# Residual quarters given back to the residual three slabs, one slab and two jobs earlier, and the last transposes one step later, in a two-layer decoder in fp32

## The chip, the core and the metric

The kernel runs on one core of a Trainium2 chip. TensorE (PE) multiplies and transposes, VectorE (DVE) and ScalarE (ACT) do the element-wise work, GpSimd (POOL) does a little of it and issues some DMAs, and SyncE (SP) issues nearly all the others. The metric is the device time of one execution, in microseconds; the profile gives the span of the recorded instructions, which is a little shorter.

## What is computed

A causal decoder trunk of two layers over 256 tokens of width 2048, all in fp32. The part that the change touches is the squared-ReLU feed-forward block at the end of each layer:

```python
def squared_relu_mlp(h, w1, w2):
    z = jax.nn.relu(h @ w1)
    return (z * z) @ w2

for i in range(DEPTH):                       # DEPTH = 2
    ...
    x = x + jnp.concatenate([token_out, mem_out], axis=-1) @ w_out[i]
    x = x + squared_relu_mlp(rms_norm(x, ffn_norm[i]), w_ff1[i], w_ff2[i])
```

`w_ff1` is 2048 x 8192 and `w_ff2` 8192 x 2048. Layer 0 mixes tokens by pooling, layer 1 by differential attention; both have a memory cross-attention.

## The kernel before

**Weights.** All large weights stand in DRAM as one array `in_w` of 725 rows of 128 x 1024, in the order in which they are used. `Feed.load` (L126) brings them in: one DMA of SP per row (L147), into a "raw" row (plain blocks, four buffers) or a "slab" row. To keep fp32 accuracy, a row is split in two: ACT casts it to fp32r (`hi`, L178), DVE subtracts that from the row (`lo`, L181), both into a ring of six half-row slots (`hi_ring`, `lo_ring`; two more slots, `slot`, in the feed-forward block). PE then makes three products of high and low parts. `_prepare` (L185) runs three preparations ahead of the matmuls, and `load` three rows ahead of that.

**Slabs.** Most of `w_ff2` (both halves A and B of its columns) is multiplied by a scheme of seven products in place of eight for a block of 2 x 2. A slab is two rows, a and b, and four jobs, j = 0 to 3 (`slab_jobs`, L1003; matmuls L1031 to L1033 into seven PSUM banks `p`). Row a needs more than a load: when it has landed, POOL issues a DMA (L149) that adds the second half of row b onto it. ACT's cast of the row comes behind that, then DVE subtracts (L209) and, for row b, adds (L212).

**Borrowed buffers.** Slab rows rotate over three buffers (tag `rows`) and over those in `feed.more`: in the feed-forward block that is the four quarters a to d of the residual (tags `resida` to `residd`), which is copied to DRAM (`kept`, L853) for that time. `load` counts rows and takes the buffer by the count modulo 3 + the number of borrowed ones. `reload` (L855) takes a quarter back and issues its DMA from `kept` (L860) on SP; like any load, that DMA first waits until the last row in this buffer has been read.

**Order of the block.** `ffn` (L835) runs up tiles (`h @ w1`, a bank `x_bank`, matmuls L940 and L942, emptied by ACT's copy at L954) with the slab jobs in between, in seven phases that alternate between the halves: the last but one, LAST-1, is half B, slabs 16 to 23, and LAST is half A, slabs 20 to 31. At the end of a phase `finish_banks` (L1047) combines the seven banks into four corners (`c_x`, `c_y` and `room`, or `c_a` and `c_b`). Corners of a phase that doesn't end its half are parked in DRAM (`part`); at LAST two DMAs (L1158) fetch them into two free places of the buffers `za` and `zb`, and DVE's L409 scales the new corners and adds the parked ones. Last, `turn(h)` transposes corners on PE (`ct`, L1100) and DVE adds them to the residual (L1103). Small pieces of such work are put off by `at(n, ...)` until n steps later; a step (`tick`) comes every four blocks.

**What sets the order.** The program is written as one sequence. The framework's scheduler sorts each engine's instructions, except those pinned to the order of the program, and each engine then runs its own queue in order: an instruction that waits holds up what stands behind it. SP's queue holds all loads, reloads, fetches and parks one behind the other.

**Places of the change.** In `go` (L1139) four of them are tied to a slab and a job: after job 3 of slab 22 of LAST-1, `feed.more` is cut to quarters c and d (L1150); after job 3 of slab 22 of LAST, a and b are reloaded (L1152); after job 3 of slab 28, borrowing ends and the parked corners are fetched (L1154); after job 1 of slab 31, c and d are reloaded (L1161). The fifth is in `finish_banks`: at LAST, `turn(h)` comes 7 + h steps later (L1117).

Of the kernel before, what the change touches and what calls it, by code (L numbers as in the profile page):

```python
# [293 lines left out]
NB = 24  # L294
# [3 lines left out]
LAST = len(PHASES) - 1  # L298
# [65 lines left out]
def program(ctx, tc, plan, dry, xT, memT, par, lam, cst, wst, yT):  # L364
# [18 lines left out]
    def at(d, fn, rank=0):  # L383
        pend.setdefault(now[0] + d, []).append((rank, fn))

    def tick():
        now[0] += 1
        for _, fn in sorted(pend.pop(now[0], []), key=lambda r: r[0]):
            fn()
# [9 lines left out]
    def bk(tag, name, shape=(P, 512)):  # L399
        return pp.tile(list(shape), F32, tag=tag, bufs=1, name=name)  # L400
# [3 lines left out]
    def mmt(name):  # L404
        turnm[0] += 1
        return bk(f"m{(turnm[0] - 1) % 3}", name)

    def stt(out, a, s, b, op0, op1, **kw):
        nc.vector.scalar_tensor_tensor(out=out, in0=a, scalar=s, in1=b, op0=op0, op1=op1, **kw)  # L409
# [425 lines left out]
    def ffn(l, xs, tag, done):  # L835
# [19 lines left out]
        def reload(tags):  # L855
            for i in tags:
                assert f"resid{i}" not in feed.lent.values()
                j = "abcd".index(i)
                resid.parts[j] = resid_part(i, f"resid{i}{l}")
                nc.sync.dma_start(resid.parts[j], kept[:, 4 * j : 4 * j + 4, :])  # L860
# [5 lines left out]
        def take():  # L866
            return spare.pop(0)
# [80 lines left out]
        def up_tile(j, ps):  # L948
            narrow(ps, "w_ff1", j, list(range(NK)), lambda k: xs[:, k, :])
            if j == 1:  # L950
                r2c.append(columns("x")[1])
                r2.append(rstd_from("x"))
                nc.scalar.activation(r2[0], r2[0], AF.Square)
            nc.scalar.copy(pairs[j // 2 % 3][:, 512 * (j % 2) : 512 * (j % 2) + 512], ps)  # L954
            if j % 2:
                convert(j // 2, (1, 1, 2, 2, 3, 4, 5, 6) if j == 63 else STEPS)
# [43 lines left out]
        def bank():  # L1000
            return pp.tile([P, 512], F32, tag="st", bufs=1, name="x_bank")
# [38 lines left out]
        def open_banks():  # L1040
            ms = [f"m{(turnm[0] + i) % 3}" for i in range(3)]
            for p, tag in enumerate((*ms, "n0", "n1", "o", "t")):
                banks.append(bk(tag, f"p{p}"))
# [3 lines left out]
        def finish_banks(p):  # L1047

            half, begin, end = PHASES[p]
            p1, p7, p6, p2, p3, p4, p5 = banks  # L1050
            banks.clear()
            if p == LAST:
                upp, low = (
                    tp.tile([P, 2, 512], F32, tag="rows", bufs=3, name=f"c_{x}") for x in "ab"
                )
                x0, x2 = upp[:, 0, :], upp[:, 1, :]
            else:
                low = room[:, 3072:4096].rearrange("p (a c) -> p a c", a=2)
                x0 = tp.tile([P, 512], F32, tag="acc2", bufs=1, name="c_x")
                x2 = tp.tile([P, 512], F32, tag="rowsq", bufs=1, name="c_y")  # L1060
            x3, x1 = low[:, 0, :], low[:, 1, :]
            corners = ((x0, x2), (x3, x1))
            add, sub = nc.vector.tensor_add, nc.vector.tensor_sub
            nc.scalar.copy(x0, p1)
            nc.scalar.copy(x1, p5)
            sub(x2, x0, p6)
            add(x3, x2, p7)
            add(x0, x0, p2)
            add(x2, x2, x1)
            add(x2, x2, p3)  # L1070
            add(x1, x1, x3)
            add(x3, x3, p4)
            whole = end == (32 if half == "A" else NB)
            sides = ((x0, 0), (x2, 1), (low, slice(2, 4)))
            old = part.pop(half, None) if p < LAST else None

            def scale():
                for side, t in ((x0, 0), (x2, 0), (low, 1)):
                    grown = nc.scalar.activation(
                        side, side, AF.Copy, scale=r2c[0][:, t : t + 1]  # L1080
                    )
                    if not dry:
                        tc.keep_in_program_order(grown)

            def gather():
                for side, c in sides:
                    nc.gpsimd.dma_start(side, old[:, c, :], accum_op=ALU.add)

            def park():
                for side, c in sides:  # L1090
                    nc.sync.dma_start(part[half][:, c, :], side)

            def turn(h):
                c = 2 * h + 8 * (half == "A")
                t4 = bk(("t", "o", "n0", "n1")[h] if half == "A" else "st", "ct", (P, 2, T))
                for e in range(2):
                    n = (2 * h + e) // 4
                    w = (2 * h + e) % 4 * P
                    for t in range(2):
                        nc.tensor.transpose(  # L1100
                            t4[:, e, t * P : t * P + P], corners[t][n][:, w : w + P], ident
                        )
                sums = nc.vector.tensor_add(resid[:, c : c + 2, :], resid[:, c : c + 2, :], t4)  # L1103
                if not dry:
                    tc.keep_in_program_order(sums)
                if half == "A":
                    done(c)
                    done(c + 1)

            if p == LAST:  # L1110
                for t, side in enumerate((upp, low)):
                    stt(
                        side, side, r2c[0][:, t : t + 1], fetched[t].bitcast(F32),
                        ALU.mult, ALU.add,
                    )
                for h in range(4):
                    at(7 + h, lambda h=h: turn(h))  # L1117
                return
            if old is not None:
                at(10, gather)  # L1120
            if not whole:
                part[half] = dp.tile([P, 4, 512], F32, tag=f"part{half}{begin}", name=f"part{l}{p}")
                at(6 if old is None else 17, park)
                if p == LAST - 2:
                    at(15, scale)
                return

            at(15, scale)
            turns.append(turn)
# [9 lines left out]
        def go(some):  # L1139
            for at_, what in some:  # L1140
                if what[0] == "s":
                    p, i, j = what[1:]
                    if not banks:
                        open_banks()
                    if (p, i) not in runs:
                        runs[p, i] = slab_jobs(p, i)
                    runs[p, i](j)
                    if at_ < first_down and at_ >= ups:
                        tick()
                    if (p, i, j) == (LAST - 1, NB - 2, 3):  # L1150
                        feed.more = feed.more[2:]
                    if (p, i, j) == (LAST, 22, 3):  # L1152
                        reload("ab")
                    if (p, i, j) == (LAST, 28, 3):  # L1154
                        feed.more = []
                        for t in range(2):
                            fetched.append(spots[take()])
                            nc.sync.dma_start(  # L1158
                                fetched[t].bitcast(F32), part["A"][:, 2 * t : 2 * t + 2, :]
                            )  # L1160
                    if (p, i, j) == (LAST, 31, 1):  # L1161
                        reload("cd")
                    continue
                if what[0] == "turn":
                    turns[0](what[1])
                    continue
                if what[0] == "end":
                    finish_banks(what[1])
                    ends[0] = True
                    continue  # L1170
                if at_ == len(items) - 3:
                    feed.extra = None
                ps = bank() if banks or ends[0] else mmt("ff")
                ends[0] = None
                if what[0] == "f":
                    up_tile(what[1], ps)
                else:
                    feed.rows_whole = False
                    down_tile(*what[1:], ps)

        first_down = items.index(("d", 3, 0))
        items = list(enumerate(items))
        go(items[:ups])

        def last():
            go(items[ups:])
            feed.rows_whole = False
# [469 lines left out]
    for c in range(3):  # L1657
# [5 lines left out]
        for i in range(2):  # L1663
            j = 2 * c + i
# [10 lines left out]
    for h in range(4):  # L1675
# [5 lines left out]
            lambda c, h=h: [mvs[:, b, c, h * P : h * P + P] for b in range(2)],  # L1681
# [110 lines left out]
```

## Time and profile before

| | |
|---|---|
| median of 3 runs | 2016.76 us (2016.6 to 2017.52) |
| the profiled execution | 2016.9 us |
| its span | 2014.8 us |
| mean granted clock of TensorE | 0.998 |
| bytes read from DRAM by the core | 430.85 MB |

The page of the profile lists each engine's busy time, then the span in slices, DMA queues, the chain of work that ended last, the costliest groups of instructions, and DMA issues with the median time to landing. In rows of instructions, the first two numbers are the start in the span and the length, in us; then follow the engine, the line, the operation, result<-source by the program's names without their numbers, and the shape; in square brackets stands the idle time of the engine just before it and what ended it. "SPq" and "POOLq" are the issues of DMAs by those engines. A group of waits reads "who waited <- for whom: total us, times, longest". A row of a stretch reads from:to and length, then busy time with the number of instructions of PE, PEld (loading of weights), DVE, ACT and POOL, then the granted clock, the share of DMA time and GB/s.

### The profile page before, as it was taken

The page shows a single profiled execution, that of the slowest core. Times are in us where ns is not written, and L with a number is a line of the kernel's source. Part 1 is how long each engine was busy: PE and PEld are TensorE (multiplying, and loading weights), DVE is VectorE, ACT ScalarE, POOL GpSimd, SP SyncE. Part 2 cuts the span into 40 slices and gives each one's busy share as a digit, 9 for nine tenths or more (in the row PEclk, how much of TensorE's full clock was granted, in tenths as well). Part 3 has the DMA queues.
Part 4 walks back from the last instruction along what each step waited for, and adds up shares of the span by engine and source line. Part 5 has one row for each costly group of instructions (what it writes and reads, how often), then busy time and mean ns, then how long its engine had stood idle before and what let it go on. Part 6 is the DMA issues. An engine that isn't in the chain of part 4 may idle for free.

```text
span 2014.8 us, 30574 instructions
## 1 busy us (share of the span) xinstructions
PE 2002.6 (99%) x10592; PEld 1708.5 (85%) x10592; DVE 1785.1 (89%) x2705; ACT 1374.1 (68%) x2213; POOL 172.2 (9%) x203
## 2 busy tenths in 40 slices
PE   9999999999999999999999999999999999999999
PEld 7888888888888888888888899888888888888787
DVE  8888779999999999999875798879999999999898
ACT  7765567676666677677665698556666666776664
POOL 0001300001011111000000000410001010011000
PEclk9999999999999999999999999999999999999999
DMA  8556768779788887766665645767778888788674
GB/s 310 183 193 213 246 206 239 233 234 265 231 252 247 238 254 233 232 195 196 222 194 190 193 142 176 241 224 231 242 226 259 239 222 269 230 258 239 197 240 149
DMA packets 139403, 452.39 MB, mean 225 GB/s; under 512 B 15792, under 2 KB 18864, under 8 KB 139248
## 3 DMA queue, kind: packets, MB, share of 16 engines
q1 hardware_dynamic: 119520, 412.68, 61.3%
q0 software_dynamic: 19584, 37.76, 11.3%
q8 instruction: 83, 1.36, 0.3%
q14 instruction: 72, 0.59, 0.1%
q10 hardware_dynamic: 144, 0.01, 0.0%
HBM read 430.85 MB, written 16.78 MB: 222 GB/s over the span
## 4 chain that ended last, share of the span: by engine, by line
PE 96%; DVE 1%; ACT 1%; DMA 1%; issue 0%; SPq 0%; ACTq 0%; DVEq 0%; POOLq 0%
PE x_bank L940 23%; PE x_bank L942 11%; PE p L1031 9%; PE p L1032 9%; PE p L1033 9%; PE wo L519 6%; PE wo L521 3%; PE q L550 3%; PE k L550 3%; PE v L550 3%; PE ff L940 3%; PE u L519 2%; PE mk L550 2%; PE mv L550 2%; PE ff L942 1%; PE u L521 1%
## 5 line engine op out<-in xcount | busy, mean ns | idle before, releaser
L181 DVE TENSOR_TENSOR lo_ring<-raw,hi_ring 128x512 fp32r<-128x512 f32 (+1 forms) x675 | 565.2, 853 | 100.0 <-ACT hi_ring L178 93.0
L178 ACT CAST hi_ring<-raw 128x512 fp32r<-128x512 f32 (+1 forms) x675 | 493.1, 745 | 228.9 <-PE wo L519 62.0
L181 DVE TENSOR_TENSOR lo_ring<-slab,hi_ring 128x1024 fp32r<-128x1024 f32 (+1 forms) x332 | 343.0, 1045 | 35.9 <-ACT hi_ring L178 32.3
L178 ACT CAST hi_ring<-slab 128x1024 fp32r<-128x1024 f32 (+1 forms) x332 | 301.0, 907 | 68.5 <-DVE slab L212 37.0
L149 POOL DMA_DIRECT2D slab<-in_w x112 | 96.9, 865 | 1631.3 <-PE o_t L1649 344.5
L940 PE MATMUL x_bank<-fx,hi_ring 128*128 128x512 f32 x720 | 227.1, 396 | 0.0
L178 ACT CAST slot<-slab 128x1024 fp32r<-128x1024 f32 (+1 forms) x116 | 120.9, 1042 | 98.3 <-PE x_bank L940 93.8
L181 DVE TENSOR_TENSOR slot<-slab,slot 128x1024 fp32r<-128x1024 f32 (+1 forms) x116 | 140.8, 1213 | 31.8 <-ACT slot L178 31.7
L942 PEld LDWEIGHTS x_bank<-fx,lo_ring 128*128 128x128 f32 x720 | 135.4, 188 | 31.6
L519 PE MATMUL wo<-cat,hi_ring 128*128 128x512 f32 x512 | 161.7, 397 | 0.0
L954 ACT COPY room<-x_bank 128x512 f32<-128x512 f32 x118 | 69.0, 584 | 133.9 <-PE x_bank L942 133.9
L940 PE MATMUL x_bank<-fx0b,hi_ring 128*128 128x512 f32 x472 | 148.3, 396 | 0.0
L942 PE MATMUL x_bank<-fx,lo_ring 128*128 128x256 f32 x720 | 141.7, 278 | 0.0
L212 DVE TENSOR_TENSOR slab<-slab,slab 128x1024 f32<-128x1024 f32 x112 | 136.8, 1221 | 0.1
L1031 PE MATMUL p<-hi_ring,zb 128*128 128x512 f32 x290 | 114.5, 395 | 2.7 <-ACT hi_ring L178 2.5
L521 PEld LDWEIGHTS wo<-cat,lo_ring 128*128 128x128 f32 x512 | 96.2, 188 | 21.8
L1033 PE MATMUL p<-lo_ring,zb 128*128 128x512 f32 x290 | 113.9, 394 | 0.5 <-DVE lo_ring L181 0.5
L940 PEld LDWEIGHTS x_bank<-fx,hi_ring 128*128 128x128 f32 x720 | 112.2, 189 | 2.5
L1032 PE MATMUL p<-hi_ring,zb 128*128 128x512 f32 x290 | 113.8, 393 | 0.0
L942 PEld LDWEIGHTS x_bank<-fx0b,lo_ring 128*128 128x128 f32 x472 | 88.8, 188 | 20.8
L521 PE MATMUL wo<-cat,lo_ring 128*128 128x256 f32 x512 | 101.8, 278 | 0.0
L942 PE MATMUL x_bank<-fx0b,lo_ring 128*128 128x256 f32 x472 | 92.8, 278 | 0.0
(550 smaller groups left out, 4676.7 us busy)
## 6 DMA issues: line engine op xcount, KB each, us to landing
raw<-in_w SPq DMA_DIRECT2D x500, 512.0 KB, 4.6
slab<-in_w SPq DMA_DIRECT2D x224, 512.0 KB, 3.8
slab<-in_w POOLq DMA_DIRECT2D x112, 256.0 KB, 4.8
part<-room SPq DMA_DIRECT2D x10, 512.0 KB, 5.0
room<-part POOLq DMA_DIRECT2D x8, 512.0 KB, 8.7
part<-c_x SPq DMA_DIRECT2D x10, 256.0 KB, 5.4
part<-c_y SPq DMA_DIRECT2D x10, 256.0 KB, 4.6
c_x<-part POOLq DMA_DIRECT2D x8, 256.0 KB, 6.5
```

The source lines that it names most:

```text
L149: self.nc.gpsimd.dma_start(t[:, 512:1024], self.wst[other, :, 512:1024], accum_op=ALU.add)
L178: cast = self.nc.scalar.copy(hi, src)
L181: self.nc.vector.tensor_sub(lo, src, hi.bitcast(F32))
L212: add(two, t.unsqueeze(1).to_broadcast([P, 2, 512]), two)
L519: nc.tensor.matmul(ps, hi, xs[:, k, :], start=first and j == 0, stop=False)
L521: nc.tensor.matmul(ps[:, T : 2 * T], lo, xs[:, k, 0:T], start=False, stop=last and j == len(ks) - 1,)
L550: nc.tensor.matmul(ps[t], a, b, start=i == 0 and j == 0, stop=i == NK - 1 and j == 2)
L940: nc.tensor.matmul(ps, hi, src(k), start=k == ks[0], stop=False)
L942: nc.tensor.matmul(ps[:, T : 2 * T], lo, src(k)[:, 0:T], start=False, stop=k == ks[-1])
L1031: nc.tensor.matmul(ps, al, hi[:, s], start=i == begin, stop=False)
L1032: nc.tensor.matmul(ps, ah, hi[:, s], start=False, stop=False)
L1033: nc.tensor.matmul(ps, ah, lo[:, s], start=False, stop=i == end - 1)
```

## The change

Five numbers; four edits in `go` and `finish_banks`. Borrowing of quarters a and b ends after slab 19 of LAST-1 and not 22, that of c and d after slab 27 of LAST and not 28; the fetch of the parked corners goes with the latter; c and d are reloaded after job 3 of slab 30 and not job 1 of slab 31, two jobs earlier; and the last turns come 8 + h steps later and not 7 + h. The reload of a and b keeps its line.

```diff
@@ finish_banks
                 for h in range(4):
-                    at(7 + h, lambda h=h: turn(h))
+                    at(8 + h, lambda h=h: turn(h))
                 return
@@ go
-                    if (p, i, j) == (LAST - 1, NB - 2, 3):
+                    if (p, i, j) == (LAST - 1, 19, 3):
                         feed.more = feed.more[2:]
                     if (p, i, j) == (LAST, 22, 3):
                         reload("ab")
-                    if (p, i, j) == (LAST, 28, 3):
+                    if (p, i, j) == (LAST, 27, 3):
                         feed.more = []
                         for t in range(2):
                             fetched.append(spots[take()])
                             nc.sync.dma_start(
                                 fetched[t].bitcast(F32), part["A"][:, 2 * t : 2 * t + 2, :]
                             )
-                    if (p, i, j) == (LAST, 31, 1):
+                    if (p, i, j) == (LAST, 30, 3):
                         reload("cd")
```

What this does to SP's queue at three places follows. Numbers behind `slab` and `raw` are the row of `in_w`; the number behind the underscore only tells tiles of one name apart.

First, layer 1, in LAST-1 and at the beginning of LAST: SP's queue in the kernel before, from a little ahead of the reloads of a and b up to the load of slab674.

```order
L147 DMA slab678_16994<-in_w 128x1024
L147 DMA slab681_17074<-in_w 128x1024
L147 DMA raw671_16840<-in_w 128x1024
L147 DMA raw672_16845<-in_w 128x1024
L860 DMA resida1_17186<-kept1_12536 128x1024
L860 DMA residb1_17188<-kept1_12536 128x1024
L147 DMA raw675_16932<-in_w 128x1024
L147 DMA raw676_16970<-in_w 128x1024
L147 DMA raw679_17004<-in_w 128x1024
L147 DMA raw680_17072<-in_w 128x1024
L147 DMA slab673_16855<-in_w 128x1024
L147 DMA raw683_17090<-in_w 128x1024
```

The next load of a slab behind these is slab674. The same stretch of SP's queue in the changed kernel:

```order
L147 DMA slab668_16763<-in_w 128x1024
L147 DMA slab673_16855<-in_w 128x1024
L147 DMA raw671_16840<-in_w 128x1024
L147 DMA raw672_16845<-in_w 128x1024
L147 DMA slab674_16900<-in_w 128x1024
L147 DMA slab677_16972<-in_w 128x1024
L147 DMA raw675_16932<-in_w 128x1024
L147 DMA raw676_16970<-in_w 128x1024
L147 DMA raw679_17004<-in_w 128x1024
L147 DMA raw680_17072<-in_w 128x1024
L147 DMA slab678_16994<-in_w 128x1024
L147 DMA raw683_17090<-in_w 128x1024
```

Slab673 now stands where slab681 stood, slab674 and slab677 where the two reloads stood, and slab678 where slab673 stood; the next load of a slab behind these is slab681. The reloads of a and b now stand fifteen rows further ahead on the queue.

Second, layer 0: the two fetches of the parked corners. SP's queue before, around the second of them:

```order
L147 DMA slab318_7617<-in_w 128x1024
L147 DMA raw317_7606<-in_w 128x1024
L147 DMA raw320_7695<-in_w 128x1024
L1158 DMA za0_2624<-part04_6230 128x1024
L147 DMA slab319_7628<-in_w 128x1024
L147 DMA slab322_7716<-in_w 128x1024
```

In the changed kernel that fetch is gone from there; the piece of the difference at its new neighbourhood, some ten rows further ahead on the same queue:

```order
 L147 DMA slab306_7351<-in_w 128x1024
 L147 DMA slab309_7428<-in_w 128x1024
+L1158 DMA zb0_2625<-part04_6230 128x1024
 L147 DMA raw311_7450<-in_w 128x1024
 L147 DMA raw312_7515<-in_w 128x1024
```

The second fetch now goes out where the first did, ahead of raw320; the first has moved to the place shown, with the loads of raw311 and raw312 behind it.

Third, the end of layer 0's block, where slab rows 323 to 331 are loaded. SP's queue before:

```order
L147 DMA raw324_7786<-in_w 128x1024
L147 DMA slab323_7729<-in_w 128x1024
L147 DMA slab326_7803<-in_w 128x1024
L147 DMA raw325_7801<-in_w 128x1024
L147 DMA raw328_7873<-in_w 128x1024
L147 DMA slab327_7815<-in_w 128x1024
L147 DMA slab330_7890<-in_w 128x1024
L147 DMA raw329_7888<-in_w 128x1024
L147 DMA raw332_7958<-in_w 128x1024
L147 DMA slab331_7900<-in_w 128x1024
L860 DMA residc0_8049<-kept0_2628 128x1024
```

And in the changed kernel:

```order
L147 DMA raw324_7788<-in_w 128x1024
L860 DMA residc0_7983<-kept0_2628 128x1024
L860 DMA residd0_7985<-kept0_2628 128x1024
L147 DMA raw325_7803<-in_w 128x1024
L147 DMA raw328_7873<-in_w 128x1024
L147 DMA slab323_7731<-in_w 128x1024
L147 DMA slab326_7805<-in_w 128x1024
L147 DMA raw329_7888<-in_w 128x1024
L147 DMA raw332_7958<-in_w 128x1024
L147 DMA slab327_7815<-in_w 128x1024
L147 DMA slab330_7890<-in_w 128x1024
```

The two reloads of c and d have moved ahead of five slab rows, each of which stands one pair of loads later than before; slab331 comes behind what is shown. In layer 1 the reloads of c and d keep their place.

## Prediction

> **What bounds the kernel now.** First the page: span and busy shares.
>
> ```profile
> span 2014.8 us, 30574 instructions
> PE 2002.6 (99%) x10592; PEld 1708.5 (85%) x10592; DVE 1785.1 (89%) x2705; ACT 1374.1 (68%) x2213; POOL 172.2 (9%) x203
> ```
>
> TensorE (PE) is the bound, and its work stays the same. Two things can be won: stretches where PE waits, and stretches where it runs slowly. The profiled execution took 2016.9 us, 2.1 more than its span; the median of the three timed runs, 2016.76, is 0.14 below it. I work against 2016.9.
>
> The change acts in the last two phases of each feed-forward block. So next, who PE waited for there: layer 0 (800 to 930 us), then layer 1 (1800 to 2015); total, times, longest.
>
> ```profile
> PE ct L1100 <- ACT room L954: 1.1, 1, 1.1
> PE ct L1100 <- DVE c_b L409: 0.5, 1, 0.5
> ```
>
> ```profile
> PE p L1031 <- ACT hi_ring L178: 2.5, 1, 2.5
> PE p L1033 <- DVE lo_ring L181: 0.5, 1, 0.5
> PE ct L1100 <- DVE c_b L409: 0.2, 1, 0.2
> ```
>
> Five waits, 4.8 us in all. The busy share hides the rest; the clock shows it. Two stretches behind the long wait (stretch, length, PE, PEld, DVE, ACT, POOL busy, granted clock, DMA share, GB/s):
>
> ```profile
> 1871.60:1878.40 6.80, 6.33 (x15) 4.36 (x15) 6.80 (x8) 5.15 (x8) 0.00 (x0) 0.50 0.14 39
> 1878.40:1890.00 11.60, 11.60 (x60) 9.85 (x59) 10.01 (x12) 9.62 (x13) 0.86 (x1) 1.00 0.70 218
> ```
>
> For 6.80 us PE runs at half the clock, and "PE busy" counts that as work.
>
> **Why PE waited.** Order of time around the wait, then the queues of SyncE (SP) and GpSimd (POOL) ahead of it:
>
> ```profile
> 1869.97 1.04 ACT L178 CAST hi_ring<-slab 128x1024 fp32r<-128x1024 f32 x1 [4.59 <-DMA slab<-in_w]
> ...
> 1871.04 1.23 DVE L181 TENSOR_TENSOR lo_ring<-slab,hi_ring 128x1024 fp32r<-128x1024 f32 x1 [4.94 <-ACT hi_ring L178]
> ...
> 1871.06 0.50 PE L1031 MATMUL p<-hi_ring,zb 128*128 128x512 f32 x1 [2.46 <-ACT hi_ring L178]
> ...
> 1872.32 0.80 PE L1033 MATMUL p<-lo_ring,zb 128*128 128x512 f32 x1 [0.47 <-DVE lo_ring L181]
> ```
>
> ```profile
> 1835.11 0.33 SPq L147 DMA_DIRECT2D slab<-in_w  x1
> ...
> 1842.23 0.33 SPq L860 DMA_DIRECT2D resida<-kept  x1
> ...
> 1858.84 0.33 SPq L147 DMA_DIRECT2D slab<-in_w  x1
> ...
> 1861.81 0.33 SPq L147 DMA_DIRECT2D slab<-in_w  x1
> ...
> 1865.24 0.86 POOL L149 DMA_DIRECT2D slab<-in_w  x1 [11.05 <-DVE room L919]
> ```
>
> Set beside the queue order shown under the change, the load at 1858.84 is slab673. It goes out only there; GpSimd adds the second row onto it from 1865.24; ACT, idle for 4.59 us, casts it at 1869.97; DVE and PE follow. The load at 1835.11 is slab681, which is needed later than slab673.
>
> **The change, part by part.**
>
> *Rows give up residual quarters a and b three slabs earlier (L1150).* In layer 1 slab673 moves on SP's queue to the place that slab681 had (1835.11), and slab674 from 1861.81 to the place of the first reload (1842.23). I take each place to keep its time, as what comes free there is set by the casts, whose order around it stays. So slab673 goes out 23.7 us earlier. I price its way by the group medians to landing:
>
> ```profile
> slab<-in_w SPq DMA_DIRECT2D x224, 512.0 KB, 3.8
> slab<-in_w POOLq DMA_DIRECT2D x112, 256.0 KB, 4.8
> ```
>
> 1835.1 + 3.8 + some 0.6 until the add goes out + 4.8 = 1844.3. PE wanted it at 1868.60 (1871.06 - 2.46), which leaves 24 us.
>
> Others pay: slab678 now goes out at 1858.84 and slab681 at 1861.81. Their casts in the trace:
>
> ```profile
> 1880.67 1.05 ACT L178 CAST hi_ring<-slab 128x1024 fp32r<-128x1024 f32 x1 [1.64 <-PE x_bank L940]
> ...
> 1889.43 1.06 ACT L178 CAST hi_ring<-slab 128x1024 fp32r<-128x1024 f32 x1 [0.30 <-PE p L1032]
> ```
>
> Even 6.4 us sooner, these come at 1874.3 and 1883.0; the data are there at 1862.6 and 1871.0 (slab681 has an add). So nothing is late next.
>
> What goes: 2.46 + 0.47 us of waiting, and half of the 6.33 us in which PE ran at clock 0.50, 3.17: **6.1**. A second way: layer 0's twin of this stage does the same 687 matmuls.
>
> ```profile
> 779.00:913.00 134.00, 132.69 (x687) 111.79 (x686) 127.17 (x167) 93.57 (x133) 8.31 (x10) 1.00 0.71 216
> 1853.70:1993.00 139.30, 136.09 (x687) 113.61 (x686) 126.30 (x163) 91.33 (x127) 8.25 (x10) 0.98 0.70 210
> ```
>
> 139.30 - 134.00 + 1.07 (a wait that layer 0 alone has, below) = 6.4. With the change ACT and DVE stand in the same order in both twins, and layer 0 has no wait at the place of layer 1's. I take **6.2**; the bounds are 2.9 (the clock doesn't recover) and 6.4.
>
> *The parked corners are fetched one slab earlier (L1154).* In layer 0 the second fetch left right behind the load of raw320:
>
> ```profile
> 842.88 0.33 SPq L147 DMA_DIRECT2D raw<-in_w  x1
> 843.30 0.38 SPq L1158 DMA_DIRECT2D za<-part  x1
> ...
> 849.31 0.62 ACT L178 CAST hi_ring<-raw 128x512 fp32r<-128x512 f32 x1 [3.46 <-DMA raw<-in_w]
> ...
> 850.47 0.33 PE L1100 MATMUL ct<-const,c_y 128*128 128x128 f32 x1 [1.07 <-ACT room L954]
> ...
> raw<-in_w SPq DMA_DIRECT2D x500, 512.0 KB, 4.6
> ```
>
> raw320 took 6.4 us where its group takes 4.6. Its cast held ACT up, so the copy that empties the bank came late and PE waited 1.07. With the fetch a slab ahead, 4.6 brings the row at 847.5, 1.8 sooner, and the copy ends before PE asks: **1.07** goes (bounds 0 and 1.07). At its new place the fetch waits until PE has read its slot for the last time, and raw311 and raw312 queue behind it:
>
> ```profile
> 820.09 1.46 SPq L147 DMA_DIRECT2D raw<-in_w  x2
> ...
> 838.63 1.99 ACT L178 CAST hi_ring<-raw 128x1024 fp32r<-128x1024 f32 x2
> ```
>
> 18.5 us lie between their issue and their casts; that covers a wait of 10 us and the contention. Cost 0.
>
> *Borrowing of quarters c and d ends a slab earlier, and they come back two jobs earlier (L1154, L1161).* In layer 0 both reloads move ahead of slabs 323 to 331, which then live on three buffers; in layer 1 they keep their place. The tightest is slab330, which now has the place of the first of these reloads (883.66):
>
> ```profile
> 883.66 0.33 SPq L860 DMA_DIRECT2D residc<-kept  x1
> ...
> 894.03 1.05 ACT L178 CAST hi_ring<-slab 128x1024 fp32r<-128x1024 f32 x1
> DMA to landing us min/median/max: 3.5/4.8/8.3
> 860.00:900.00 40.00, 40.00 (x206) 33.99 (x205) 39.58 (x60) 29.43 (x46) 1.72 (x2) 1.00 0.69 218
> ```
>
> 883.7 + 3.8 + 0.6 + 4.8 = 892.9, 1.1 us ahead of its cast: cost 0 at the median. At the 8.3 of the slowest add it is 2.4 late, and DVE, with 0.42 us idle in 40, can't catch up. That is the thin spot.
>
> *Last turns one step later (L1117).* The same 16 transposes and four sums per layer, later by a step. In layer 1:
>
> ```profile
> L1103 DVE TENSOR_TENSOR residd<-residd,ct x4: 680/683/689, 921.1 to 2002.3; 128x512 f32<-128x512 f32 x4
> L983 DVE TENSOR_TENSOR residb<-residb,room x1: 425/425/425, 2011.4 to 2011.4; 128x256 f32<-128x256 f32 x1
> ```
>
> The last sum at 2002.3 can come later by 8 us before it meets the kernel's last one, at 2011.4; that work hides it, and a step is shorter. The waits for c_b (0.5 and 0.2) stay, since the transposes still follow DVE's L409; bounds -0.7 and +0.5. I take 0.
>
> **Sum:** 6.2 + 1.1 = 7.3; 2016.9 - 7.3 = **2009.6 us**.
>
> **The rivals.**
>
> *DVE sets the pace.* It was 4.94 us idle in the long wait, less than the 6.2 that PE is to win, and is 99% busy in 860 to 900. If DVE has no reserve up to the corners, PE wins 4.94 in layer 1, and layer 0's 1.07 turns up again before the c_b transposes: 2016.9 - 4.9 = 2012.0. Against it: over the twin, DVE is idle 13.0 us in layer 1 (139.30 - 126.30), 6.8 in layer 0, and layer 0 runs without the long wait.
>
> *The add is late in layer 0's end: slower.* With three buffers, slab330's add takes 8.3 us instead of 4.8, and each of its two neighbours (slab326, slab327) loses as much: 3 x 2.4 = 7.2 us on DVE, hence on PE, and a half-clock stretch behind (3.2): 10.4 - 7.3 = 3.1 slower, 2020.0; with a second such stretch 2023. It decides once adds there take over 5.9 us (4.8 + 1.1). For it: 8.3 occurred. Against: the median is 4.8, and DMA share is only 0.69 there.
>
> *The slow clock has another cause.* Then only the waits go: 2.93 + 1.07 = 4.0, 2012.9. The trace has one such stretch, starting within 1 us of the wait, and the twin has neither; that speaks against. The Trainium skill ("TensorE: Matmul & The Clock Gate", Part 1: The HAM clock gate) lets the clock halve after at least one idle window of about 3.4 us. By that rule 2.46 us of idle, 0.79 of work and 0.47 of idle need not have done it; the measured 0.50 right behind this wait weighs more.
>
> *The change doesn't reach PE.* Slab673 is loaded early, but its add stays late, since POOL waits for something else (its 11.05 us are put down to DVE). Then only 1.07 goes: 2015.8. Against: the load went out 6.4 us ahead of that add and takes 3.8 to 6.
>
> **How the numbers follow.** A measurement of this kernel can tell about 0.2%, 4.0 us: below 2012.7 is faster, above 2020.8 slower. Forecast 0.68 (2008.8 to 2011); DVE 0.14; late adds 0.09, of which 0.05 above 2020.8; the clock 0.04; not reaching PE 0.05. Faster: 0.68 and 0.12 of the DVE case, 0.80. Slower: 0.05. Within: 0.15. The low end takes all five waits and the twin's 6.4: 6.4 + 1.07 + 0.5 + 0.2 = 8.2, and 0.4 for the spread of the runs: 2008.3. The high end takes in the DVE case and the clock, 2013.0; 0.14 lie above.
>
> **What would show it.** Right: no PE wait over 0.5 us between 1853 and 1985, clock 1.00 throughout, the load of slab673 near 1835; no PE wait at 849; layer 1's twin stage near 133. Wrong: a wait of ACT for a slab between 870 and 900, a second half-clock stretch, or a c_b wait of over 1 us in layer 0.

## The result, and the profile after

The changed kernel takes 2008.64 us (median of 6 runs, 2008.34 to 2009.8), the kernel before 2017.14 us in its 6 runs; the ratio is 0.9958, with a 95% interval of 0.9945 to 0.9971. The profiled execution took 2008.8 us, 8.1 less than that of before. First the page of the profile after: span and busy times of the engines.

```profile
span 2006.7 us, 30584 instructions
## 1 busy us (share of the span) xinstructions
PE 1999.1 (100%) x10592; PEld 1706.5 (85%) x10592; DVE 1783.4 (89%) x2705; ACT 1374.5 (68%) x2213; POOL 171.4 (9%) x203
```

Both the busy time of PE and the rest of the span have shrunk: 3.5 us less "busy" for the same 10592 matmuls (most of it the half clock, which the forecast had priced at 3.17), and 4.6 us less waiting. Who PE waited for, in layer 0 (800 to 930 us) and then in layer 1 (1800 to the end); total, times, longest:

```profile
PE ct L1100 <- DVE c_b L409: 0.5, 1, 0.5
...
PE ct L1100 <- DVE c_b L409: 0.2, 1, 0.2
```

Of the five waits of before, the two for `c_b` are left, within 0.02 us of what they were; the two behind slab673 and the one at raw320 are gone. The stage of layer 1, from the first job of LAST to the wait for `c_b`, at its new place (columns as before):

```profile
1852.46:1984.75 132.29, 132.23 (x687) 111.88 (x686) 125.75 (x162) 91.20 (x127) 8.23 (x10) 1.00 0.74 224
```

The clock is 1.00 throughout. By exact marks (the end of PE's work ahead of the first job of LAST, and the end of its work ahead of the wait for `c_b`), the execution divides like this; the last column adds up to the 8.1:

| stretch, us | before | after | saved |
|---|---|---|---|
| start to LAST of layer 0 | 779.04 | 778.67 | 0.37 |
| LAST of layer 0 | 133.84 | 132.24 | 1.60 |
| from there to LAST of layer 1 | 940.83 | 941.56 | -0.73 |
| LAST of layer 1 | 139.15 | 132.28 | 6.87 |
| the rest | 21.99 | 21.97 | 0.02 |

I put the first and third rows down to no edit, which is not shown. The start has waits that differ from trace to trace. A wait at 1325 us, ahead of layer 1's first up tile, is under 0.15 us in the traces of the kernel before and of three experiments, 0.38 us here, and 0.22 to 1.14 in the other experiments. The two stages of LAST do the same work in both layers, and now they take the same time.

The way of slab673, read from SP's queue, POOL's, ACT and PE:

```profile
1833.87 0.33 SPq L147 DMA_DIRECT2D slab<-in_w  x1
...
1837.94 0.86 POOL L149 DMA_DIRECT2D slab<-in_w  x1 [8.97 <-DVE room L915]
...
1861.15 1.05 ACT L178 CAST hi_ring<-slab 128x1024 fp32r<-128x1024 f32 x1
...
1867.21 0.40 PE L1031 MATMUL p<-hi_ring,zb 128*128 128x512 f32 x1
```

The load leaves at 1833.87 where it left at 1858.84 before, the add leaves at 1837.94, and the cast has no idle time before it: it comes 6.06 us ahead of the matmul that needs it. Before, it came 1.09 ahead (1869.97 and 1871.06), straight after the data. And raw320 in layer 0, on ACT and PE:

```profile
847.30 0.63 ACT L178 CAST hi_ring<-raw 128x512 fp32r<-128x512 f32 x1 [1.81 <-DMA raw<-in_w]
847.83 0.58 ACT L954 COPY room<-x_bank 128x512 f32<-128x512 f32 x1
...
848.88 0.27 PE L1100 MATMUL ct<-const,c_y 128*128 128x128 f32 x1
```

ACT still waits for this load, but only 1.81 us and not 3.46; the copy ends at 848.41, and the transpose at 848.88 shows no wait.

### The profile page after: what moved, and what is told of

The parts are those of the page before. It is cut to its first block, busy times and chain, and to the rows that moved or that the text cites. A ratio compares the mean times of both kernels' runs of the same rounds, so it can differ in the third digit from the quotient of the medians.

```text
span 2006.7 us, 30584 instructions
## 1 busy us (share of the span) xinstructions
PE 1999.1 (100%) x10592; PEld 1706.5 (85%) x10592; DVE 1783.4 (89%) x2705; ACT 1374.5 (68%) x2213; POOL 171.4 (9%) x203
## 4 chain that ended last, share of the span: by engine, by line
PE 98%; DVE 1%; DMA 1%; ACT 0%; issue 0%; SPq 0%; ACTq 0%
PE x_bank L940 23%; PE x_bank L942 12%; PE p L1031 9%; PE p L1032 9%; PE p L1033 9%; PE wo L519 6%; PE q L550 3%; PE k L550 3%; PE ff L940 3%; PE v L550 3%; PE wo L521 3%; PE u L519 2%; PE mk L550 2%; PE mv L550 2%; PE ff L942 1%; PE u L521 1%
## 5 line engine op out<-in xcount | busy, mean ns | idle before, releaser
L212 DVE TENSOR_TENSOR slab<-slab,slab 128x1024 f32<-128x1024 f32 x112 | 136.5, 1219 | 0.1
L1031 PE MATMUL p<-hi_ring,zb 128*128 128x512 f32 x284 | 111.3, 392 | 0.3
L1032 PE MATMUL p<-hi_ring,zb 128*128 128x512 f32 x284 | 110.9, 391 | 0.0
```

Source lines behind the costliest of these rows:

```text
L212: add(two, t.unsqueeze(1).to_broadcast([P, 2, 512]), two)
L1031: nc.tensor.matmul(ps, al, hi[:, s], start=i == begin, stop=False)
L1032: nc.tensor.matmul(ps, ah, hi[:, s], start=False, stop=False)
```

## The experiments

Theory: two late loads cost the time. Slab673 in layer 1 (cured by L1150) makes the long wait and the half clock behind it; raw320 in layer 0, slowed by the fetch right behind it (cured by L1154), makes the shorter one. The rivals: the turns or the c and d edits are needed; the half clock has another cause; and, on the other side, that the new arrangement stands close to a loss.

### L1150 alone

```diff
-                    if (p, i, j) == (LAST - 1, NB - 2, 3):
+                    if (p, i, j) == (LAST - 1, 19, 3):
```

> Only the edit at L1150 (borrowing of quarters a and b ends after slab 19 of LAST-1, not 22). Theory 'late row' (slab673 loaded behind the reloads of a and b makes both PE waits and the half clock behind them): the whole loss of layer 1's stage goes with this edit alone. The stage from 1853.7 (first job of LAST) to the c_b wait took 139.15 us before and 132.29 after the whole change; expected here 132.3, no PE wait over 0.1 us in it but c_b's, clock 1.00 throughout; time 6.9 us below the kernel before, some 2010. Layer 0 stays at 133.8 with its wait of 1.07. Rival 'order of the other engines' (the gain needs the turns or the c and d edits as well): a PE wait of 0.5 us or more is left between 1853 and 1985. Rival 'clock has another cause': waits gone, but a stretch at clock 0.50 near 1870 remains, stage 135.5.

Measured: 2011.12 us (7 runs) against 2016.99 (16 runs of the kernel before), ratio 0.9969 (0.9958 to 0.9981). The long wait and the half clock are gone, but layer 1's stage takes 134.40 us, not 132.3. ACT and PE there, in this run:

```profile
1925.17 0.62 ACT L178 CAST hi_ring<-raw 128x512 fp32r<-128x512 f32 x1 [4.04 <-DMA raw<-in_w]
1925.69 0.58 ACT L954 COPY room<-x_bank 128x512 f32<-128x512 f32 x1
...
1926.33 0.33 PE L1100 MATMUL ct<-const,c_y 128*128 128x128 f32 x1 [1.64 <-ACT room L954]
```

This is layer 0's wait once more, in layer 1: the row is raw704, the twin of raw320 (384 rows on), and on SP's queue a fetch stands right behind its load:

```profile
1917.03 1.46 SPq L147 DMA_DIRECT2D raw<-in_w  x2
1918.59 0.38 SPq L1158 DMA_DIRECT2D za1a<-part  x1
```

So the expectation fell for the whole gain, though not for the wait at slab673. In this trace 4.75 of layer 1's 6.87 us come with L1150 alone; the rest needs the fetch moved too. The trace is of the slowest of the seven executions, 2012.98 us (the others took 2009.46 to 2012.35): by the medians, L1150 alone saves 5.9 us and L1154 alone, below, 2.2. How much raw704 cost in the executions that have no trace isn't known.

### L1154 alone, and the fetch alone

First the edit at L1154 alone:

```diff
-                    if (p, i, j) == (LAST, 28, 3):
+                    if (p, i, j) == (LAST, 27, 3):
                         feed.more = []
                         for t in range(2):
```

> Only the edit at L1154 (borrowing of c and d ends, and the parked corners are fetched, after slab 27 and not 28). Theory 'fetch ahead of raw320': raw320 lands about 1.6 us sooner after its issue (4.7 us in place of 6.35), the ct wait of 1.07 in layer 0 goes, and the small stall of weight loads behind it (0.48 us) too: layer 0's stage 132.2 in place of 133.8. Layer 1 stays as before (waits of 2.46 and 0.47, half clock, stage 139.2). Time 1.6 us below the kernel before, within what a measurement can tell. Rival 'the turns one step later took the wait away': the wait at 849 stays within 0.3 of 1.07, stage 133.8.

Then only the fetch earlier, with the end of borrowing where it was:

```diff
-                    if (p, i, j) == (LAST, 28, 3):
-                        feed.more = []
+                    if (p, i, j) == (LAST, 27, 3):
                         for t in range(2):
...
+                    if (p, i, j) == (LAST, 28, 3):
+                        feed.more = []
```

> The fetch of the parked corners after slab 27, but borrowing of c and d still ends after slab 28, all else as before. Theory 'fetch ahead of raw320': as with the whole edit, the ct wait of 1.07 in layer 0 goes and its stage is 132.2 (within 0.3). Rival 'it is the rows given back, not the fetch': the wait stays. Layer 1 as before, 139.2.

Measured: 2014.76 us (10 runs), ratio 0.9988 (0.9978 to 0.9997), and 2013.12 us (one run). In both, layer 0's stage takes 132.23 us and PE waits there for nothing but `c_b` (0.5). So it is the place of the fetch that counts. Layer 1, which was expected at 139.2, took 139.45 in the first run and 137.07 in the second. PE's waits for slab673 there, of the first run and of the second:

```profile
PE p L1031 <- ACT hi_ring L178: 3.0, 1, 3.0
PE p L1033 <- DVE lo_ring L181: 0.5, 1, 0.5
```

```profile
PE p L1031 <- ACT hi_ring L178: 2.2, 1, 2.2
PE p L1033 <- DVE lo_ring L181: 0.3, 1, 0.3
```

The second run's two waits are 1.1 us shorter in all, yet it gains 2.4 us on the first. The other difference is the clock: half for 6.83 us in the first run and for 3.41 us in the second. The stretches around it in the second (granted clock is the third number from the end):

```profile
1866.05:1869.46 3.41, 1.19 (x7) 0.89 (x6) 0.33 (x1) 1.41 (x2) 0.00 (x0) 1.00 0.38 70
1869.46:1872.87 3.41, 3.12 (x8) 1.51 (x6) 3.41 (x5) 1.75 (x4) 0.00 (x0) 0.50 0.00 0
1872.87:1876.28 3.41, 3.41 (x15) 2.64 (x15) 3.41 (x4) 3.41 (x5) 0.00 (x0) 1.00 0.24 71
```

Eight matmuls in the half-clock cell, 15 in the next, at the same "busy" time: that is what the half clock costs.

### Both edits, the other two edits, and one slab instead of three

Both edits together:

```diff
-                    if (p, i, j) == (LAST - 1, NB - 2, 3):
+                    if (p, i, j) == (LAST - 1, 19, 3):
...
-                    if (p, i, j) == (LAST, 28, 3):
+                    if (p, i, j) == (LAST, 27, 3):
```

> The edits at L1150 and L1154 together, the other two (c and d reloaded two jobs earlier, turns one step later) left out. From the run with L1150 alone: layer 1's stage was 134.4, not 132.3, since a ct wait of 1.64 appeared at raw704, layer 1's twin of raw320 (6.9 us from issue to landing, with a fetch right behind it). Theory 'two late rows, twice': with the fetch moved too, both stages take 132.2 to 132.3, no PE wait over 0.1 but those for c_b, clock 1.00, and the time equals that of the whole change, 2008.6 within 0.2%. Rival 'the other two edits matter': a wait of 0.3 us or more that the whole change doesn't have, or a stage over 132.6.

Only the other two:

```diff
-                    at(7 + h, lambda h=h: turn(h))
+                    at(8 + h, lambda h=h: turn(h))
...
-                    if (p, i, j) == (LAST, 31, 1):
+                    if (p, i, j) == (LAST, 30, 3):
```

> Only the reload of c and d after job 3 of slab 30 and the turns one step later; the edits at L1150 and L1154 left out. Theory: nothing changes. Layer 0's stage 133.8 with a ct wait of about 1.1 at raw320; layer 1's 139.2 with waits of about 2.5 and 0.5 and the half clock. Rival: either stage shorter by 0.5 us or more.

Both edits, but with L1150 at slab 21:

```diff
-                    if (p, i, j) == (LAST - 1, NB - 2, 3):
+                    if (p, i, j) == (LAST - 1, 21, 3):
...
-                    if (p, i, j) == (LAST, 28, 3):
+                    if (p, i, j) == (LAST, 27, 3):
```

> As the edits at L1150 and L1154 together, but borrowing of a and b ends after slab 21, one slab earlier than before and not three. Slab673 then stands ahead of the reloads already. Theory 'late row': one slab is enough, slab673's data are there 10 us or more ahead of its cast, and both stages take 132.2 to 132.4. Rival 'three are needed': slab673 or a neighbour is late, a PE wait of 0.5 us or more in layer 1's stage.

Measured: both edits, 2008.93 us (5 runs), ratio 0.9961 (0.9947 to 0.9975), stages 132.23 and 132.21, no wait but those for `c_b`: the whole gain. The other two alone, 2018.74 us (one run), with layer 1's stage at 140.33 and slab673's wait at 3.11 us. Layer 0's stage was 133.08, 0.76 under the kernel before, which is over the 0.5 that I had set as the rival's mark. But the wait at raw320 is still there (0.33), and raw704's has come up in layer 1 (1.15): what differed is how long the two loads took, 5.61 and 6.43 us (next table). With slab number 21, 2008.63 us (one run) and stages of 132.23 and 132.13. So one slab earlier is enough, and no version was faster than the change by more than a measurement can tell; slab673 was there 39.4 us ahead of its cast, against 18.5 in the changed kernel.

Put beside each other, these runs show what raw320 and raw704 cost. Landing is the time from SP's issue to the landing of the data, by the trace's records of DMAs; "excess" is the stage over 132.24 us, where slab673 plays no part in it:

| run, layer | what stands right behind the load | landing, us | PE's wait | excess |
|---|---|---|---|---|
| L1150 alone, 1 | fetch | 6.92 | 1.64 | 2.16 |
| L1150 alone, 0 | fetch | 6.62 | 1.34 | 1.89 |
| the other two, 1 | fetch | 6.43 | 1.15 | |
| before, 0 | fetch | 6.35 | 1.07 | 1.60 |
| the other two, 0 | fetch | 5.61 | 0.33 | 0.84 |
| before, 1 | fetch | 5.13 | 0 | |
| the changed kernel, 0 and 1 | slab row | 4.70, 4.81 | 0, 0 | 0, 0.04 |
| both edits, 0 and 1 | slab row | 4.78, 4.68 | 0, 0 | -0.01, -0.03 |

In every row with a wait, it is the landing less 5.28 us; the excess is the landing less 4.73 to 4.77. The 0.5 us between them show in no wait of a matmul: DVE, behind ACT, is late with the next row too, and PE's weight load waits for that. Of the kernel before, layer 0, and then the same place in layer 1, where raw704 held up no matmul:

```profile
854.40 0.30 PEld L942 LDWEIGHTS x_bank<-fx0a,slot 128*128 128x128 f32 x2 [0.48 <-DVE slot L181]
...
1934.42 0.30 PEld L942 LDWEIGHTS x_bank<-fx,slot 128*128 128x128 f32 x2 [0.49 <-DVE slot L181]
```

In the changed kernel these two waits are 0.12 and 0.23 us. So raw704 was late in layer 1 of the kernel before as well. By the table its 5.13 us cost 0.4 there, an estimate: 5.13 less 4.73 to 4.77.

### Does a wait bring the half clock?

The changed kernel, with ACT held up at six up tiles; `ident` holds zeros and ones and keeps its values.

```diff
         def up_tile(j, ps):
+            for _ in range({(0, 16): 20, (0, 30): 26, (0, 44): 32, (1, 16): 36, (1, 30): 42, (1, 44): 50}.get((l, j), 0)):
+                held = nc.scalar.copy(ident, ident)
+                if not dry:
+                    tc.keep_in_program_order(held)
```

> The changed kernel with ACT held up at six places, by 20, 26, 32 (layer 0) and 36, 42, 50 (layer 1) copies of the 128 x 128 identity onto itself, each some 0.27 us, ahead of up tiles 16, 30 and 44 of the feed-forward block; nothing else is changed. PE waits for casts there, for about as long as the hold is longer than the three preparations that ACT is ahead: expected waits from about 0 at 20 copies (5.4 us) to some 6 us at 50 (13.5 us). Theory 'a PE wait brings the half clock': behind waits of 2.5 us or more PE runs at clock 0.50 for some 6 to 7 us; behind short waits of under 1 us it doesn't. Rival 'the half clock at 1871.6 had another cause': clock 1.00 behind all of them. A third outcome: only waits over some length longer than 2.46 do it, and then the stretch at 1871.6 needs another reason.

Measured: waits of 3.02, 4.58, 6.56, 8.32, 9.86 and 12.49 us, and behind (or still in) each of them a stretch at clock 0.50, of 6.83, 6.83, 6.83, 10.24, 13.65 and 13.65 us. There is no other such stretch between the start and the end. The first and the last, each with the cells before and behind it:

```profile
386.71:390.12 3.41, 1.21 (x6) 0.66 (x4) 0.69 (x1) 3.22 (x11) 0.86 (x1) 1.00 0.48 79
390.12:396.95 6.83, 5.73 (x13) 4.07 (x14) 5.44 (x6) 3.97 (x5) 0.00 (x0) 0.50 0.09 21
396.95:400.36 3.41, 3.41 (x20) 2.93 (x19) 3.08 (x4) 1.41 (x2) 0.00 (x0) 1.00 0.98 298
...
1789.58:1793.00 3.42, 1.51 (x8) 0.92 (x6) 0.00 (x0) 3.17 (x11) 0.00 (x0) 1.00 0.30 57
1793.00:1796.41 3.41, 0.00 (x0) 0.00 (x0) 0.00 (x0) 3.06 (x12) 0.00 (x0) 1.00 0.00 0
1796.41:1810.07 13.66, 6.45 (x14) 4.24 (x15) 6.16 (x7) 10.11 (x24) 0.00 (x0) 0.50 0.11 38
```

The rival that the half clock at 1871.6 had nothing to do with the wait falls: six waits that were put in brought six such stretches. All lengths are multiples of 3.413 us, and within a run all of them begin and end on one grid of that width.

> The changed kernel with shorter holds of ACT: 14, 16, 17 (layer 0) and 12, 14, 15 (layer 1) copies of the identity ahead of up tiles 16, 30, 44. From the longer holds (0.26 us per copy; 20 copies gave 3.02): PE waits of about 1.5, 2.0, 2.2 and 1.7, 2.2, 2.5 us. All half-clock stretches so far begin on a grid of 3.413 us and last 1 to 4 of its cells; the cell ahead of each held 1.97 to 3.41 us of PE waiting, while cells with 1.64 and 1.91 were not followed by one. Theory 'cells': a wait is followed by the half clock only if 1.95 us or more of it lie in one cell, so waits of 1.5 to 1.7 never bring it, and of those of 2.0 to 2.5 the ones that a cell's border cuts don't either. Rival 'length alone': every wait over some length brings it, wherever it lies.

The same edit, with the shorter holds. Measured: the waits came out shorter than expected (1.05, 1.27, 1.62, 0, 0.58 and 0.94 us for the slots' casts), and one of them was followed by the half clock, the 1.62 at 675.81:

```profile
675.39:678.80 3.41, 1.73 (x7) 0.79 (x6) 1.58 (x3) 1.98 (x6) 0.00 (x0) 1.00 0.07 12
678.80:682.21 3.41, 3.41 (x8) 2.17 (x9) 3.38 (x4) 2.81 (x4) 0.00 (x0) 0.50 0.01 2
682.21:685.63 3.42, 3.42 (x19) 2.91 (x18) 3.39 (x4) 1.82 (x2) 0.00 (x0) 1.00 0.84 285
```

So the 1.95 of my theory is wrong, and the rival "length alone" is too: the run with L1150 alone has a wait of 1.64 us, cut into 0.97 and 0.67 by a border at 1925.65 (25 cells before the half clock that sets in at its end, 2010.98), and no half clock behind it. The cell 1789.58 to 1793.00 above, with 1.91 us of waiting, was not followed by one either. Whether a cell halves the next isn't sorted by its waiting time alone; what else goes in is open.

### How close is the new arrangement to a loss?

The forecast named the add of slab330, at the end of layer 0, as the thin spot. In the changed kernel:

| row | landed ahead of its cast, us |
|---|---|
| slab323, 326, 327, 330, 331 (layer 0) | 1.71, 1.87, 3.69, 1.67, 1.60 |
| slab714 (layer 1, twin of slab330) | 0.45 |

Two kernels hold those two adds back. The first:

```diff
             if r[0] == "S" and r[2] == 0:
+                for _ in range({330: 24, 714: 60}.get(h, 0)):
+                    junk = self.wpool.tile([P, 32], F32, tag="junk", bufs=1, name="junk")
+                    self.nc.gpsimd.tensor_mul(junk, t[:, 0:32], t[:, 0:32])
```

> The changed kernel with the adds of two rows held back: GpSimd makes 24 small products (128 x 32, into a scratch tile) of the landed row ahead of the add of slab330, at the end of layer 0, and 60 ahead of the add of slab714, its twin in layer 1; how long these take is read from the trace, some 0.2 us each, 5 and 12 us. In the changed kernel the two rows land 1.67 and about 1.2 us ahead of their casts. The prediction's price for a late add: what is over the slack falls on DVE and hence on PE at full length, some 3 us of PE waiting at slab330 and 10 at slab714. Rival 'lead': casts stand about 6 us ahead of the matmuls that use them (slab673: cast at 1861.15, matmul at 1867.21), so a delay of under slack + 6 us costs PE nothing or under 1 us at slab330, and some 12 - 7 = 5 us at slab714, with a half clock behind it.

Measured: 2026.87 us, but not for the expected reason. A product took 0.55 us, and the scheduler let the add pass all products but the first, so the rows came in time; it was DVE's subtraction (here L212, as lines have moved by 3), which overwrites what the products read, that waited:

```profile
899.44 0.69 DVE L212 TENSOR_TENSOR slab<-slab 128x512 f32<-128x512 f32 x1 [3.62 <-POOL junk L151]
```

DVE's 3.62 us made layer 0's stage 3.7 us longer (135.94): DVE has no reserve there, as the forecast had it. In layer 1, with its 60 products, the stage took 146.57, with a PE wait of 11.38 us. The run says nothing on late adds. In the second, 8 and 20 products read the half of the row that the add writes:

```diff
+                for _ in range({330: 8, 714: 20}.get(h, 0)):
...
+                    self.nc.gpsimd.tensor_mul(junk, t[:, 512:544], t[:, 512:544])
```

> The changed kernel with the adds of slab330 (layer 0) and slab714 (layer 1) held back by 8 and 20 small products on GpSimd; they now read the half of the row that the add writes, so the add cannot pass them, and nothing else waits for them. In the run before this one a product took 0.55 us, so the adds go out 4.4 and 11 us later; the rows had 1.67 and about 1.2 us of slack, so their casts come 2.7 and 9.8 us late. The prediction's price: that falls on DVE and PE at full length, layer 0's stage 132.2 + 2.7 = 134.9, layer 1's 132.3 + 9.8 = 142.1 with a half clock on top. Rival 'lead of ACT': a cast stands about 6 us ahead of its matmul, so the first costs PE under 0.5 us and the second about 4 us. The run before this one, in which DVE itself was held 3.6 us at slab330 and layer 0's stage took 3.7 us longer, speaks for the first.

Measured: 2019.34 us. Counted from the beginning of the stage, the cast of slab330 comes 4.08 us later than in the changed kernel, that of slab714 9.16. PE's waits in the two stages, layer 0 (885 to 915 us) and layer 1 (1970 to 1997):

```profile
PE ct L1103 <- DVE c_b L412: 0.9, 1, 0.9
PE p L1036 <- DVE slot L184: 0.5, 1, 0.5
PE p L1034 <- ACT slot L181: 0.4, 1, 0.4
PE ct L1103 <- DVE c_a L412: 0.4, 1, 0.4
PE p L1036 <- DVE lo_ring L184: 0.3, 1, 0.3
```

```profile
PE p L1034 <- ACT hi_ring L181: 3.1, 1, 3.1
PE ct L1103 <- DVE c_b L412: 0.9, 1, 0.9
PE ct L1103 <- DVE c_a L412: 0.4, 1, 0.4
```

Layer 0's stage takes 135.16 and the wait for `c_b` 0.47 more than in the changed kernel: 3.4 of the 4.08 us fall on PE. Layer 1's takes 139.67 and `c_b` 0.78 more: 8.2, of which two half-clock cells are 3.4. Neither theory has it whole. The cast's own lead takes up 6 us, as the rival said (9.16 late, 3.10 waited; and at slab330 no wait for that cast at all), but what is late on DVE stays late to the end of the stage, and comes out in several small waits.

The last kernel lengthens the stretch on three buffers:

```diff
-                    if (p, i, j) == (LAST, 27, 3):
+                    if (p, i, j) == (LAST, 25, 3):
```

> The changed kernel with borrowing of c and d ending, and the parked corners fetched, after slab 25 of LAST and not 27; the reload after slab 30 stays. On SP's queue both fetches then leave side by side some ten rows ahead, and in layer 1 the reloads of c and d move ahead of five slab rows, as they already did in layer 0. Theory: three buffers keep up, the rows arrive 1 to 2 us ahead of their casts for as long as the stretch lasts; both stages 132.2 to 132.5, no new wait. Rival 'the cover runs out': slack falls from slab to slab, a cast waits for an add, PE waits 0.5 us or more in a stage.

Measured: 2009.5 us, stages 132.85 and 132.79. Of slab rows 703 to 715 in layer 1, five land 0.96 to 2.67 us ahead of their casts, but slab714 only 0.07 (its cast waited for it) and slab715 0.33. No PE wait reaches 0.2 us. The 0.6 us in each stage fit raw320 and raw704, which landed after 5.38 and 5.46 us (less 4.77: 0.61 and 0.69); no fetch stands behind them here: next comes, 5.25 us later, a slab row behind raw320 and a reload behind raw704. Why they were slower than in the table's last rows isn't known. Three buffers keep up, without a reserve.

## Why the prediction was right, point by point

- **The sum.** Forecast 2009.6, measured 2008.64; 7.3 us between the profiled executions, 8.1 measured. The mechanism held, and both terms were sized too small. The result lies just below the 2008.8 to 2011 of the forecast's own case, and that it lies inside the whole range was partly luck: the low end, 2008.3, counted on 0.7 us of waits for `c_b`, which stayed. Without them it would have been 2009.0.
- **Quarters a and b (L1150), 6.2 with bounds 2.9 and 6.4.** The stage gave 6.87, above the upper bound. The waits (2.46, 0.47 and one of 0.07 at 1934.42, behind raw704) and the half clock, 3.17, make 6.17 of it. Of the other 0.7, some 0.3 is raw704's, by the estimate of 0.4 above; what is left may be catching up behind the waits, which the trace doesn't split up. More important, in the trace with L1150 alone only 4.75 of the 6.87 came: the step that failed is "a wait that layer 0 alone has". Layer 1 was spared a wait of a matmul because raw704 happened to land in 5.13 us, 0.15 under the mark of 5.28, with a fetch right behind it as in layer 0. In the traces with L1150 alone and with the other two edits it landed in 6.92 and 6.43, and PE waited. The forecast priced L1150 by itself too high for such an execution; the total came out because the other edit moves the fetch in both layers.
- **The fetch (L1154), 1.07 with bounds 0 and 1.07.** The reason held: with the fetch moved and nothing else, raw320 took 4.57 us. In the changed kernel it took 4.70, where the group median of 4.6 was put in. At its new place the fetch went out at 819.11 and the two raw rows behind it at 819.86, so it cost nothing, as forecast. The size is 1.60 in layer 0: I counted the matmul's wait and missed DVE's delay behind it, 0.5 us, which only a wait of PE's weight load shows.
- **Rows that go later.** Right: nothing became late. Slab678 and slab681 landed 10.0 and 11.4 us ahead of their casts (11.7 and 12.0 by the forecast's sum).
- **Quarters c and d, cost 0.** Right. Slab330 had 1.67 us where I had worked out 1.1. The thinnest row was another: slab714, which this edit doesn't move, with 0.45.
- **Last turns, cost 0.** Right: the waits for `c_b` are 0.46 and 0.16, before 0.48 and 0.18, and both edits without this one and the c and d reload give the same stages.
- **The rivals.** That DVE sets the pace fell: DVE did layer 1's stage in 132.29 us with 6.5 us to spare. That the clock had another cause fell, by the holds of ACT. That the add stays late fell: it left 0.56 us after the row had landed at 1837.38. The slower side, late adds, didn't come up; its price, full length on DVE and PE, was too high: 3.4 of 4.08 came in layer 0, and 4.8 of 9.16 in layer 1, beside 3.4 of half clock.

## What to carry to other kernels

A load that a borrowed buffer delays should be looked up in the queue of the engine that issues it: for slab673 the place there, not the transfer's length, decided when it came, and one slab's difference was enough. Two stages that do the same work are each other's yardstick, but a wait that only one of them shows may be missing from the other by luck: ask how far its load was from being late before you leave it out. And where PE is the bound, a wait can cost more than it shows: the 2.46 and 0.47 us here had 3.17 us of half clock behind them, and raw320's wait of 1.07 came to 1.60 with what DVE still had to catch up.

## What the runs showed of the hardware

The half clock comes in cells of 3.413 us on a grid that runs through a whole execution: stretches of 3.41, 6.83, 10.24 and 13.65 us, each beginning at a border. So in two kernels that differ in the place of one statement, waits of 2.22 and 3.05 us had one and two half-clock cells behind them. By estimate such a cell costs 1.7 us, half its length, beside the wait itself: above, eight matmuls ran in one and 15 in the next. The Trainium skill ("TensorE: Matmul & The Clock Gate", Part 1: The HAM clock gate) speaks of a free-running window of about 3.4 us, which agrees with the grid; it lets the clock fall after a whole window of idle time, and there the runs differ: cells with 1.19, 1.21 and 1.73 us of PE's work in them were followed by clock 0.50.

A DMA that is issued after a load can slow that load: raw320 and raw704, with the fetch issued 0.4 us behind them, took 5.1 to 6.9 us in six cases, and 4.6 to 4.8 in the eighteen cases in which the traces of the changed kernel and of the other experiments have no fetch there and the next issue of SP comes some 5 us later. The run with the fetch at slab 25 is the exception: no fetch stands there either, and the two rows took 5.38 and 5.46. GpSimd's add went out 1.0 us behind them there, in most other traces about 2; but it did so behind raw704 in the changed kernel too, which took 4.81. So the fetch isn't the only thing that slows them; what the other is, and what makes the spread from 5.1 to 6.9, isn't known.
